# Dense products of a split float32 weight: the weights' low part as the last pass of each half block

## The chip, the cores and the metric

The kernel runs on one core of one Trainium2 chip. The metric is the device time of one execution in microseconds, over several runs, as their median. Engines are named as the profile names them: PE is TensorE (PEld its weight loads), DVE VectorE, ACT ScalarE, POOL GpSimd, SP SyncE, which issues nearly all DMAs.

## The reference

Two transformer-like blocks run one after the other on 512 positions of 2048 channels. The first has a depthwise convolution branch and a differential attention branch; the second mixes a gated delta rule (GDN, 8 heads) and an RWKV-7 recurrence (16 heads, in pairs) over a context of 256 positions and then over the 512 latent positions. Cut to what matters here:

```
p = h @ w_in[l]                                   # block 1, all projections
x = x + gate * rms_norm((sig*y_conv + sig*y_attn) @ w_o[l], g_post[l])
u  = h  @ w_in_2 ;  uc = hc @ w_in_2              # block 2: latent and context
ya_c, ya = gdn_mixer(uc[..., :GDN_COLS], u[..., :GDN_COLS], ...)
yb_c, yb = rwkv_mixer(uc[..., GDN_COLS:], u[..., GDN_COLS:], ...)
x = x + gate * (concat([ya, yb]) @ w_out)
```

Everything is float32, and the kernel keeps that accuracy in its large products.

## The kernel before

All activations are stored with channels on the 128 partitions and positions along the free axis. A dense output of 128 channels by T positions (T is 512, or 256 for the context) is one call of `mblock` (lines 129 to 136): it takes one PSUM bank from the pool `pd`, which has two, and calls `products` once for each **half block** of eight input blocks of 128 channels. `products` (lines 139 to 158) loads the half block's weights into `wraw` (three buffers), and splits them: ACT copies them to `whi`, rounded to the fast matmul type fp32r (line 105), and DVE subtracts to get the rest, `wlo` (line 106). `whi` and `wlo` have two buffers each. The activations exist as the same kind of pair (`ah`, `al`), made earlier. Then come three matmuls for each of the eight input blocks, `whi*ah`, `whi*al`, `wlo*ah`, 24 in all, accumulated in one PSUM bank (line 157). In the stage of the context's dense GDN products `K.on_pool` is 2, so every second `wlo` is made by POOL in place of DVE.

The program is written in Python once and its order on each engine is set by a list scheduler ahead of time; each engine then runs its list strictly in order and waits on semaphores. The scheduler takes, of the instructions that its own plan holds to be ready, the one with the lowest priority number, which is by default the place in the program. Two things bend that. In `products` every matmul whose number n in the accumulation is not a multiple of `K.burst` (12 in the first part, 6 from the end of block 1 on) gets a priority that puts it ahead of all else, so dense products come in bursts of 6 or 12 and other PE work can only come in between bursts. And the class `Visit` (lines 113 to 126) does the same for the few matmuls of one step of a recurrence. So the dense products of the next head fill PE while the recurrence of the present head waits for DVE or ACT.

The stages, by the time in the profile: the first products of block 1, in six banks at once and a quarter of the inputs at a time (`block1_h`, up to about 145 us); convolution and gates (to 435); the context's dense GDN products (`ctx_dense_gdn`, to about 626); the context's recurrences and block 1's attention (to 1780); block 1's output products (to 2150); the latent GDN stage (`mixers_gdn`, about 2240 to 3000); the latent RWKV stage (`mixers_rwkv`, to about 3620); output products and the final norm.

The GDN recurrence of one head (`gdn_core`, line 735 on) is four steps, each a chain of three handovers between PE and DVE: PE multiplies the state (`pc<-S,gk`), DVE makes `gd_R` (line 747), PE multiplies (`pc<-gd_R,gd_uu`), DVE makes `gd_vn` (line 755), PE multiplies (`pc<-gd_vn,gd_ktl` and four matmuls into `po` for the output), DVE makes the next state `S` (line 775).

Of the kernel before, what the change touches and what calls it, by code (L numbers as in the profile page):

```python
# [103 lines left out]
def split(K, hi, lo, src, eng=None):  # L104
    K.nc.scalar.copy(hi, src)  # L105
    (eng or K.nc.vector).tensor_tensor(lo, src, hi.bitcast(F32), op=ALU.subtract)  # L106


FIRST = 1000000
# [22 lines left out]
def mblock(K, wap, act, T, k0=0, k1=16, half=8):  # L132

    ps = K.pd.tile([128, 512], F32, name="pd")
    for ka in range(k0, k1, half):
        products(K, ps, wap, act[ka - k0:], T, ka, min(half, k1 - ka), k0, k1)
        K.fill()
    return ps[:, :T]


def products(K, ps, wap, act, T, ka, w, k0, k1):


    nc, tc = K.nc, K.tc
    raw = K.wp.tile([128, 8, 128], F32, name="wraw")
    hi = K.wp.tile([128, 8, 128], F32R, name="whi", bufs=2)
    lo = K.wp.tile([128, 8, 128], F32R, name="wlo", bufs=2)
    nc.sync.dma_start(raw[:, :w], wap[:, ka:ka + w, :])
    K.n_split += 1
    split(K, hi[:, :w], lo[:, :w], raw[:, :w], nc.gpsimd if K.on_pool and K.n_split % K.on_pool == 0 else nc.vector)  # L150
    for k in range(w):
        ah, al = act[k]
        for j, (a, b) in enumerate(((hi, ah), (hi, al), (lo, ah))):
            n = 3 * (ka - k0 + k) + j
            ahead = FIRST if n % K.burst else 0
            tc.cur_priority -= ahead
            nc.tensor.matmul(ps[:, :T], lhsT=a[:, k], rhs=b, start=(n == 0), stop=(n == 3 * (k1 - k0) - 1))  # L157
            tc.cur_priority += ahead


def rsqrt(K, pool, src, shape, a, eps, name, eng=None, exact=False):
# [196 lines left out]
def inv64(K, pool, upool, nm, ds, px, tmp):  # L358
# [30 lines left out]
    for lev in range(2):  # L389
        yp, zp = products()  # L390
        ys = pool.tile([128, n, 32], F32, name="iv_y")
        for m in range(n):
            for r in range(4):
                q = slice(32 * r, 32 * r + 32)
                o = 32 * (r % 2)
                nc.tensor.matmul(yp[q, m], lhsT=nm[q, m, o:o + 32], rhs=t32[q, m], start=True, stop=True,
                                 tile_position=(32 * r, 32 * r))
        nc.scalar.copy(ys, yp)
        for m in range(n):
            for r in range(4):  # L400
                q = slice(32 * r, 32 * r + 32)
                nc.tensor.matmul(zp[q, m], lhsT=ys[q, m], rhs=u32[q, m], start=True, stop=True,  # L402
                                 tile_position=(32 * r, 32 * r))
        for d, m0, w in orders:
            nc.vector.copy_predicated(u32[:, m0:m0 + w], K.cp[d, lev].unsqueeze(1).to_broadcast([128, w, 32]),  # L405
                                      zp[:, m0:m0 + w])
        nc.vector.transpose(t32.rearrange("p n e -> p (n e)"), u32.rearrange("p n e -> p (n e)"))

    u64 = upool.tile([128, n, 64], F32, name="iv_u64")
    for b in range(2):  # L410
        nc.vector.tensor_scalar(u64[:, :, 32 * b:32 * b + 32], u32, c["m64"][:, b:b + 1], None, op0=ALU.mult)
    yp, zp = products()
    ys = pool.tile([128, n, 32], F32, name="iv_y")

# [1432 lines left out]
```

## Time and profile before

| | us |
|---|---|
| median of 3 runs | 3961.03 |
| lowest and highest | 3956.98 and 3964.54 |
| the profiled execution's own time | 3948.75 |
| its span, first to last instruction | 3947.0 |
| PE busy in it | 3672.7 |
| DVE busy in it | 2748.4 |
| ACT busy in it | 1359.4 |
| POOL busy in it | 505.4 |

The profile shows one execution. Matmuls overlap: a product of 512 columns is shown with about 0.39 us, though one starts every 0.23 us. "Idle before" is the time in which an engine had nothing to run, and its releaser is what ended that time. A tile name stands for all its buffers. In the profile the two names before a matmul's size are the tensor that moves and the one that is loaded as weights, so `pd<-big,wlo` is a product of the weights' low part with an activation in `big`, and `hc` holds the context's activations.

### The profile page before, as it was taken

To read this page: it belongs to the slowest core of one execution; us is meant where nothing else is said; L and a number is where in the kernel's file an instruction comes from. 1 tells how busy PE (TensorE), PEld (TensorE's weight loads), DVE (VectorE), ACT (ScalarE), POOL (GpSimd) and SP (SyncE) were. 2 spreads that over 40 slices of the span, in tenths; PEclk is the share of its full clock that TensorE was granted. 3 is DMA by queue.
4 is the path that set the end of the run, shared out by engine and by line. 5 is a ranking of instruction groups with operands and counts; after the bars stand their busy time and mean duration, and the time that the engine had idled before them with its cause. 6 is when DMAs were issued, how large, how long until landed. Compare 5 with 4: busy or idle time off the path is not lost. (4 is left out here: it accounts for less than half of the span.)

```text
span 3947.0 us, 81802 instructions
## 1 busy us (share of the span) xinstructions
PE 3672.7 (93%) x33066; PEld 2837.3 (72%) x33066; DVE 2748.4 (70%) x7146; ACT 1359.4 (34%) x2713; POOL 505.4 (13%) x595
## 2 busy tenths in 40 slices
PE   8899878999999999999998889989999999998997
PEld 4577678876777777777886577777877777766676
DVE  3366798788778778553524877776767778877866
ACT  3322333323334344332322432322323444444333
POOL 0100231003101001000311201100001111111102
PEclk9999899999999999999999999999999999999998
DMA  8766445423433333425523222222223122212235
GB/s 321 269 226 216 161 133 173 140 102 127 136 118 107 118 111 126 130 81 179 204 93 129 101 88 68 67 69 75 86 79 110 65 68 81 68 67 83 91 129 203
DMA packets 206491, 492.95 MB, mean 125 GB/s; under 512 B 40096, under 2 KB 71328, under 8 KB 202016
## 3 DMA queue, kind: packets, MB, share of 16 engines
q1 hardware_dynamic: 206112, 487.72, 36.4%
q8 instruction: 260, 4.26, 0.4%
q14 instruction: 119, 0.97, 0.1%
HBM read 434.54 MB, written 53.09 MB: 124 GB/s over the span
## 5 line engine op out<-in xcount | busy, mean ns | idle before, releaser
L157 PE MATMUL pd<-big,whi 128*128 128x512 f32 x5280 | 1759.5, 411 | 8.0 <-ACT big L352 8.0
L157 PEld LDWEIGHTS pd<-big,whi 128*128 128x128 f32 x5280 | 964.4, 192 | 251.4 <-issue 20.8
L157 PE MATMUL pd<-big,wlo 128*128 128x512 f32 x2768 | 1104.2, 399 | 24.3 <-DVE wlo L106 23.6
L105 ACT CAST whi<-wraw 128x1024 fp32r<-128x1024 f32 (+2 forms) x498 | 502.9, 1010 | 1159.5 <-PE pd L157 1074.7
L106 DVE TENSOR_TENSOR wlo<-wraw,whi 128x1024 fp32r<-128x1024 f32 (+2 forms) x478 | 572.9, 1199 | 318.4 <-ACT whi L105 311.2
L157 PEld LDWEIGHTS pd<-big,wlo 128*128 128x128 f32 x2768 | 530.0, 191 | 147.1 <-DVE wlo L106 28.2
L157 PE MATMUL pd<-hc,whi 128*128 128x256 f32 x1152 | 227.0, 297 | 11.5 <-ACT hc L352 5.5
L157 PE MATMUL pd<-hc,wlo 128*128 128x256 f32 x576 | 171.7, 298 | 33.0 <-DVE wlo L106 23.9
L157 PEld LDWEIGHTS pd<-hc,whi 128*128 128x128 f32 x1152 | 188.3, 199 | 15.3 <-ACT hc L352 5.6
L157 PE MATMUL pd<-ext,whi 128*128 128x512 f32 x512 | 184.6, 401 | 3.8 <-DVE ext L106 3.8
L1160 DVE SCALAR_TENSOR_TENSOR cv_y<-cv_up,vec,cv_y 128x512 f32<-128x512 f32 x240 | 180.9, 754 | 4.2
L157 PE MATMUL pd<-fa,whi 128*128 128x512 f32 x448 | 149.9, 414 | 0.9 <-ACT fa L105 0.8
L157 PEld LDWEIGHTS pd<-hc,wlo 128*128 128x128 f32 x576 | 114.8, 199 | 40.0 <-DVE wlo L106 28.0
L944 POOL TENSOR_TENSOR rg_bk<-rg_th,rg_L 64x512 f32<-64x512 f32 x48 | 69.1, 1439 | 400.5 <-ACT rg_L L923 274.0
L1055 ACT ACTIVATE rg_zw<-rg_H,rg_wc 64x64 f32<-64x64 f32 x320 | 102.8, 342 | 43.4 <-DVE rg_H L1077 39.2
L157 PEld LDWEIGHTS pd<-ext,whi 128*128 128x128 f32 x512 | 97.3, 190 | 27.9 <-DVE ext L106 4.7
L1077 DVE SCALAR_TENSOR_TENSOR rg_H<-pc,rg_wc,rg_zw 64x64 f32<-64x64 f32 x320 | 90.4, 282 | 33.7 <-PE pc L123 24.0
L567 DVE SCALAR_TENSOR_TENSOR gc_y<-gc_up,vec,gc_y 128x512 f32<-128x512 f32 (+1 forms) x160 | 108.6, 679 | 2.8 <-issue 0.2
L242 DVE SCALAR_TENSOR_TENSOR ada_ev<-wraw,cs_ada,ada_ev 128x512 f32<-128x512 f32 x120 | 93.7, 781 | 20.3 <-DMA wraw<-in_wada_dram 18.9
L157 PEld LDWEIGHTS pd<-fa,whi 128*128 128x128 f32 x448 | 80.7, 190 | 21.8 <-ACT fa L105 1.9
L157 PE MATMUL pd<-fa,wlo 128*128 128x512 f32 x224 | 89.1, 398 | 0.7 <-DVE wlo L106 0.7
L405 DVE COPY_PREDICATED iv_u<-cpi,px 128x256 f32<-128x256 int32 (+2 forms) x112 | 35.2, 340 | 73.2 <-PE px L402 62.8
(589 smaller groups left out, 5592.9 us busy)
## 6 DMA issues: line engine op xcount, KB each, us to landing
wraw<-in_w_dram SPq DMA_DIRECT2D x366, 512.0 KB, 3.6
wraw<-in_wada_dram SPq DMA_DIRECT2D x128, 512.0 KB, 4.5
wraw<-in_wada_dram SPq DMA_DIRECT2D x32, 1024.0 KB, 4.8
wraw<-in_wo_dram SPq DMA_DIRECT2D x32, 512.0 KB, 3.5
sgl<-sgd SPq DMA_DIRECT2D x48, 256.0 KB, 3.3
wraw<-in_wout_dram SPq DMA_DIRECT2D x20, 512.0 KB, 3.8
wraw<-in_w_dram SPq DMA_DIRECT2D x36, 256.0 KB, 3.6
sgd<-msg SPq DMA_DIRECT2D x32, 256.0 KB, 3.3
```

The lines of the kernel that those rows point to most:

```text
L105: K.nc.scalar.copy(hi, src)
L106: (eng or K.nc.vector).tensor_tensor(lo, src, hi.bitcast(F32), op=ALU.subtract)
L157: nc.tensor.matmul(ps[:, :T], lhsT=a[:, k], rhs=b, start=(n == 0), stop=(n == 3 * (k1 - k0) - 1))
L242: nc.vector.scalar_tensor_tensor(ev, raw[:, k], cs[:, kk, 0:1], ev, op0=ALU.mult, op1=ALU.add)
L405: nc.vector.copy_predicated(u32[:, m0:m0 + w], K.cp[d, lev].unsqueeze(1).to_broadcast([128, w, 32]), zp[:, m0:m0 + w])
L567: nc.vector.scalar_tensor_tensor(y, up[:, t:t + T], w[:, t:t + 1], y, op0=ALU.mult, op1=ALU.add)
L944: nc.gpsimd.tensor_tensor(bk[uq, :, u], th[uq], F[uq], op=mul)
L1055: nc.scalar.activation(zw[hv[u], d], H[hv[u], ms[d], u], AF.Copy, scale=wn[hv[u], 4 * d + mn])
L1077: nc.vector.scalar_tensor_tensor(Hn[hv[u], 4 * d + mn, u], pc3[hv[u], 2, d], wn[hv[u], 4 * d + mn], zw[hv[u], d], op0=mul, op1=ALU.add)
L1160: nc.vector.scalar_tensor_tensor(y, up[:, t:t + 512], w[:, t:t + 1], y, op0=ALU.mult, op1=ALU.add)
```

## The change

In `products` the loop over input blocks with three products each is replaced by one list: first `whi*ah` and `whi*al` for every input block, then `wlo*ah` for every input block. Products, operands and their number stay the same; so do loads, splits and buffers. The number n still counts through the list, so a burst ends after the same number of matmuls. The new matmul stands at line 156.

```diff
-    for k in range(w):
-        ah, al = act[k]
-        for j, (a, b) in enumerate(((hi, ah), (hi, al), (lo, ah))):
-            n = 3 * (ka - k0 + k) + j
-            ahead = FIRST if n % K.burst else 0
-            tc.cur_priority -= ahead
-            nc.tensor.matmul(ps[:, :T], lhsT=a[:, k], rhs=b, start=(n == 0), stop=(n == 3 * (k1 - k0) - 1))
-            tc.cur_priority += ahead
+    n = 3 * (ka - k0)
+
+    for a, k, b in [(hi, k, b) for k in range(w) for b in act[k]] + [(lo, k, act[k][0]) for k in range(w)]:
+        ahead = FIRST if n % K.burst else 0
+        tc.cur_priority -= ahead
+        nc.tensor.matmul(ps[:, :T], lhsT=a[:, k], rhs=b, start=(n == 0), stop=(n == 3 * (k1 - k0) - 1))
+        tc.cur_priority += ahead
+        n += 1
```

What the scheduler makes of it is seen in the order of instructions. First, PE in the context's dense GDN products, around a norm's `px<-gc_th` matmul. Before:

```order
L157 MATMUL pd<-hc,whi 128x256 x2
L157 MATMUL pd<-hc,wlo 128x256
L157 MATMUL pd<-hc,whi 128x256 x2
L157 MATMUL pd<-hc,wlo 128x256
L260 MATMUL px_4296<-gc_th,cst 128x256
L157 MATMUL pd<-hc,whi 128x256 x2
L157 MATMUL pd<-hc,wlo 128x256
```

and with the change:

```order
L156 MATMUL pd<-hc,whi 128x256 x16
L156 MATMUL pd<-hc,wlo 128x256 x8
L260 MATMUL px_4296<-gc_th,cst 128x256
L156 MATMUL pd<-hc,whi 128x256 x16
L156 MATMUL pd<-hc,wlo 128x256 x8
```

The first product that needs `wlo` stands 17th in a half block and no longer third; the other work of this stage stands where it stood.

Second, DVE in the latent GDN stage, second head, where `wlo` is made. Before, the head's `wlo` stands 27 rows behind the `gd_R` of the next head's first step, after `gd_dd`, `iv_tmp` and the output norm; the rows around it:

```order
L377 STREAM_SHUFFLE iv_sh<-iv_u_23237 128x32
L565 TENSOR_SCALAR gc_y<-gc_up,vec 128x512
L378 TENSOR_TENSOR iv_sh<-iv_sh,iv_n_23235 128x32
L106 TENSOR_TENSOR wlo<-wraw,whi 128x1024
L379 TENSOR_TENSOR iv_u_23237<-iv_u_23237,iv_sh 128x32
```

With the change:

```order
L747 SCALAR_TENSOR_TENSOR gd_R_23531<-pc,TM_lat,gd_vt 128x128
L173 SCALAR_TENSOR_TENSOR go_rs_t<-go_rs_y 128x4
L567 SCALAR_TENSOR_TENSOR gc_y<-gc_up,vec,gc_y 128x512
L174 TENSOR_TENSOR go_rs_t<-go_rs_t,go_rs_xh 128x4
L106 TENSOR_TENSOR wlo<-wraw,whi 128x1024
L175 SCALAR_TENSOR_TENSOR go_rs_y<-go_rs_t,go_rs_y 128x4
```

One `wlo` now stands four rows behind that `gd_R`, ahead of `gd_dd`, `iv_tmp` and the output norm.

Third, PE in the recurrence of the third head, from the outputs of the first step on. Before:

```order
L123 MATMUL po<-gd_egt,S_0_5734 128x128
L157 MATMUL pd<-big,whi 128x512 x2
L157 MATMUL pd<-big,wlo 128x512
L157 MATMUL pd<-big,whi 128x512 x2
L157 MATMUL pd<-big,wlo 128x512
L123 MATMUL pc<-S_23550,gk 128x128
L123 MATMUL pc<-S_23548,gk 128x128
L309 MATMUL px_23759<-cst,gn_rs_y 4x128
L157 MATMUL pd<-big,whi 128x512 x2
L157 MATMUL pd<-big,wlo 128x512
L157 MATMUL pd<-big,whi 128x512 x2
L157 MATMUL pd<-big,wlo 128x512
```

With the change:

```order
L123 MATMUL po<-gd_egt,S_0_5734 128x128
L123 MATMUL pc<-S_23550,gk 128x128
L123 MATMUL pc<-S_23548,gk 128x128
L123 MATMUL pc<-gd_R_23559,gd_uu 128x128
L123 MATMUL pc<-gd_R_23557,gd_uu 128x128
L309 MATMUL px_23759<-cst,gn_rs_y 4x128
L315 MATMUL px_23762<-gc_th,cst 128x128 x2
L123 MATMUL pc<-gd_vn_23566,gd_ktl 128x128
L123 MATMUL pc<-gd_vn_23564,gd_ktl 128x128
```

In this head the dense products stand in one longer run ahead of the recurrence, and its handovers follow each other without a burst between them.

## Rows read from the trace of the kernel before

**Rows 1.** The page's parts 1 and 2: busy time, and slices of PE and its clock.
```profile
PE 3672.7 (93%) x33066; PEld 2837.3 (72%) x33066; DVE 2748.4 (70%) x7146; ACT 1359.4 (34%) x2713; POOL 505.4 (13%) x595
...
PE   8899878999999999999998889989999999998997
...
PEclk9999899999999999999999999999999999999998
```
**Rows 2.** The page's part 5, dense products of `wlo`, by the activation's tile.
```profile
L157 PE MATMUL pd<-big,wlo 128*128 128x512 f32 x2768 | 1104.2, 399 | 24.3 <-DVE wlo L106 23.6
...
L157 PE MATMUL pd<-hc,wlo 128*128 128x256 f32 x576 | 171.7, 298 | 33.0 <-DVE wlo L106 23.9
```
**Rows 3.** Waits of PE, whole span: us in total, times, longest us.
```profile
PE pd L157 <- DVE wlo L106: 48.1, 24, 4.5
...
PE pd L157 <- POOL wlo L106: 8.8, 14, 2.0
...
PE pc L157 <- DVE wlo L106: 0.6, 1, 0.6
...
PE px L157 <- DVE wlo L106: 0.5, 1, 0.5
```
**Rows 4.** Windows: the context's dense GDN stage and the latent GDN stage.
```profile
456.00:626.00 170.00, 134.58 (x976) 126.69 (x975) 148.58 (x290) 60.41 (x95) 56.08 (x57) 0.94 0.41 134
...
2240.00:3000.00 760.00, 712.11 (x6708) 578.62 (x6707) 549.14 (x1640) 227.57 (x400) 70.89 (x165) 0.97 0.25 82
```
**Rows 5.** Waits of PE from 456 to 626 us.
```profile
PE pd L157 <- DVE wlo L106: 23.6, 15, 4.3
```
**Rows 6.** Waits of PE from 2240 to 3000 us.
```profile
PE pd L157 <- DVE wlo L106: 22.6, 5, 4.5
PE pc L123 <- DVE gd_vn L755: 7.1, 6, 1.2
```
**Rows 7.** Timeline of PE in a latent GDN head: start, us, instruction.
```profile
2405.31 0.63 PE L157 MATMUL pd<-big,whi 128*128 128x512 f32 x2
2405.78 0.39 PE L157 MATMUL pd<-big,wlo 128*128 128x512 f32 x1
2406.01 0.63 PE L157 MATMUL pd<-big,whi 128*128 128x512 f32 x2
2406.47 0.39 PE L157 MATMUL pd<-big,wlo 128*128 128x512 f32 x1
...
2410.06 0.73 PE L157 MATMUL pd<-big,whi 128*128 128x512 f32 x2
2415.30 0.79 PE L157 MATMUL pd<-big,wlo 128*128 128x512 f32 x1 [4.50 <-DVE wlo L106]
...
2416.74 0.63 PE L157 MATMUL pd<-big,wlo 128*128 128x512 f32 x1
...
2418.02 0.59 PE L157 MATMUL pd<-big,wlo 128*128 128x512 f32 x1
```
**Rows 8.** Timelines of ACT and DVE around the same wait.
```profile
2408.85 1.04 ACT L105 CAST whi<-wraw 128x1024 fp32r<-128x1024 f32 x1 [0.90 <-PE pd L157]
...
2414.03 1.22 DVE L106 TENSOR_TENSOR wlo<-wraw,whi 128x1024 fp32r<-128x1024 f32 x1
```
**Rows 9.** Windows behind that wait: PE's instructions (x7) and granted clock 0.50.
```profile
2415.30:2418.40 3.10, 3.10 (x7) 2.47 (x8) 3.10 (x9) 0.00 (x0) 0.00 (x0) 0.50 0.53 176
```
**Rows 10.** Timelines of DVE and POOL in the context's dense GDN stage.
```profile
558.74 0.42 DVE L174 TENSOR_TENSOR gn_t<-gn_t,gn_xh 128x256 f32<-128x256 f32 x1
...
561.33 2.50 DVE L174 TENSOR_TENSOR gn_t<-gn_t,gn_xh 128x256 f32<-128x256 f32 x1
...
560.34 3.21 POOL L106 TENSOR_TENSOR wlo<-wraw,whi 128x1024 fp32r<-128x1024 f32 x1 [1.24 <-ACT whi L105]
```
**Rows 11.** Timeline of PE, a GDN handover with no product between.
```profile
2386.75 0.61 PE L123 MATMUL pc<-gd_R,gd_uu 128*128 128x128 f32 x4
2388.53 0.71 PE L123 MATMUL pc<-gd_vn,gd_ktl 128*128 128x128 f32 x4 [1.18 <-DVE gd_vn L755]
```
**Rows 12.** Timeline of PE at the start of a stage whose activations are just being split.
```profile
1789.18 0.79 PE L157 MATMUL pd<-ext,whi 128*128 128x512 f32 x1 [3.77 <-DVE ext L106]
```

## Prediction

> **What bounds the kernel.** I read the page's parts 1 and 2 first. PE is busy 93% of the span, and near 9 tenths in most slices; no other engine comes near [rows 1]. So time is saved where PE stops, or where its clock falls. Next came the costliest groups: there the products of `wlo` carry nearly all idle time of the dense products, 24.3 us for the latent ones and 33.0 us for the context's [rows 2]. The waits of PE agree: it stood 48.1 us in 24 stops for a `wlo` of DVE, 8.8 us in 14 for one of POOL, and 1.1 us more, 58.0 us in all [rows 3]. That is 1.5% of the span, and the most that the change can hand back directly.
>
> Then I asked where these stops lie. Two stages hold 55.0 of the 58.0 us: the context's dense GDN products (23.6 us for DVE's, and POOL's 8.8) [rows 3, 5] and the latent GDN stage, where five stops take 22.6 us [rows 6]. These two are not alike. In the latent stage PE is busy 712.1 of 760 us and DVE 549.1; in the context's stage it is the other way round, PE 134.6 of 170 us and DVE 148.6 [rows 4]. What a removed stop is worth must be read from each.
>
> A third thing is the price of a stop beyond itself. In a steady run a `wlo` product stands every 0.69 to 0.70 us, 0.23 us per product; behind the stop of 4.50 us they stand 1.28 and 1.44 us apart, 0.43 to 0.48 us per product [rows 7]. The granted clock there is 0.50, which is the 1.2 GHz level, and PE did nothing ahead of it for the length of the stop [rows 7, 9].
>
> **The change part by part.** It adds and removes no instruction, and no load or split. What it moves is when `wlo` is first needed, when `whi` is free again, and, through the scheduler, the order on all engines.
>
> *Latent GDN, the stops.* PE came to the third product of a half block, while ACT had cast `whi` at 2408.85 and DVE made `wlo` only at 2414.03, behind its other work in the queue [rows 8]. Now 16 products need `whi` alone, so `wlo` may be 14 products later: 14 x 0.23 = 3.2 us. The other 1.3 us of a stop should go too, as the order shows a `wlo` far earlier in DVE's list, and `whi` is released after two thirds of a half block. I take all five stops: -22.6 us [rows 6].
>
> *Latent GDN, the clock.* Seven matmul records ran at the low clock behind each stop [rows 9]. Each cost 0.43 - 0.23 = 0.20 us more, so 5 x 7 x 0.20 = -7.0 us.
>
> *Latent GDN, the handovers.* This speaks against the change. In the order of this stage I count 185 runs of dense products before and 157 with the change, for almost the same number of products (1926 and 1902). PE has fewer places where a burst covers a handover of the recurrence to DVE and back. Handovers without a product between go from 17 to 39, 22 more. A bare one cost 1.18 us of PE's time [rows 11], and six of that kind 7.1 us [rows 6]. Of the 22, four more have nothing between; the others have two to five small matmuls, or the output's four, in the gap. From below such a one costs 0: before, eleven handovers of this kind left no row among this stage's longer waits, where the six empty ones did [rows 6]; from above it costs 1.18 us. I take 1.18 us for four and half, 0.6 us, for 18: 4.7 + 10.8 = +15.5 us, between 4.7 and 26.0. On the other side a run that starts anew costs about 0.10 us (its first two products 0.73 us, in a run 0.63) [rows 7], and 28 fewer starts give -2.8 us. The stage comes to -22.6 - 7.0 + 15.5 - 2.8 = -16.9 us.
>
> *Context's dense GDN.* PE's 32.4 us of stops lie beside a DVE that idles only 170 - 148.6 = 21.4 us [rows 4], and every handover of the stage passes DVE. So no more than 21.4 us can come back here as long as DVE's work keeps its length, and none need to, if DVE only waits elsewhere. I take half, -10.7 us. What holds DVE is seen in one row: a `gn_t` multiplication of 0.42 us took 2.50 us while POOL made a `wlo` for 3.21 us [rows 10], and nothing here takes that away. The Trainium skill says on its page "SBUF — State Buffer", section "Who interferes with whom", that VectorE's second SBUF input comes through a read interface shared with GpSimd, and that such instructions contend. The row agrees: the time lost is DVE's, not PE's, and by that rule alone this stage would give 0 and the sum come out 10.7 us later.
>
> *The remaining stops*: 58.0 - 22.6 - 32.4 = 3.0 us, in many places [rows 3]; I take them all, -3.0 us.
>
> *Starts of stages.* Where activations are split just ahead of the products, as at 1789.18, where PE waited 3.77 us for one [rows 12], the last activation is now followed by 2 + 8 products of its half block instead of 3: 7 x 0.23 = 1.6 us later. The four chunks of block 1's first products and the four ahead of the latent stage have half that many products, and others of the same chunk beside them. I take +4.0 us for all, between 0 and 8.
>
> *SP, the DMAs and POOL*: a half block's load moves by a few places in SP's list, and is hidden by the two half blocks that its third buffer holds ahead; without that cover it would show as a wait for `wraw`, which no row here has. POOL makes the same 20 `wlo`, with the two small `gc_up` fills behind each as before. 0 for both.
>
> The sum is -16.9 - 10.7 - 3.0 + 4.0 = -26.6 us. Against the profiled execution's 3948.75 us that is 3922.2 us. That execution lies 12.3 us (0.3%) below the median of the runs shown, 3961.03 us, and under the lowest of them; the runs are what the change is compared with, so the forecast is 3961.03 - 26.6 = 3934 us.
>
> **The rivals.**
> - *Everything comes back.* The bare handovers cost little, since the small matmuls in them fill the gap, and DVE's idle time is all used: -22.6 - 7.0 + 4.7 - 2.8 - 21.4 - 3.0 = -52.1 us, 3909 us. For it: 18 of the 22 have something between. Against it: DVE already stood between PE's two matmuls in the one bare handover that I can read [rows 11].
> - *DVE bounds the context's stage and the handovers are dear.* GDN gives -22.6 - 7.0 + 26.0 - 2.8 = -6.4, the context's stage 0, remaining stops -3.0, starts +4.0: -5.4 us, 3956 us, within what can be told from no change. For it: DVE's held `gn_t` [rows 10], and PE's price in [rows 11].
> - *Slower: DVE's queue paces a bare recurrence.* In the third and fifth head the recurrence now runs from the first step's output to its end without products, while DVE's list still has 0.7 to 1.2 us instructions, a `wlo` of 1.22 us among them [rows 8], between the links. If a handover then costs its 1.18 us and one such instruction, 2.4 us, the 22 cost 52.8 us. The stage gives +20.4 us, the starts 8.0, the context's stage and the rest nothing: +28.4 us, 3989 us. It decides from about (22.6 + 7.0 + 2.8) / 22 = 1.5 us per handover in this stage. Against it: the row of 1.18 us already has DVE's other work in it, as five of its kind came out the same [rows 6].
> - *The change does not do what it says*: ruled out for the context's stage by the order; in six-bank work bursts are mixed with those of other banks, but `wlo` stands late there too.
>
> **How the numbers follow.** I give the forecast (from -45 to -10 us) 0.62, everything back 0.10, the dear handovers with DVE as bound 0.18, slower 0.10. The predicted time is the likeliest, 3934 us. The range reaches from a little beyond everything back, 3902 us, to a little beyond the case without a gain, 3964 us; outside lie the slower rival and some of the first, about 0.15. A difference under 0.2%, 8 us, can't be told from no change here. Faster by more than that hold the forecast, the first rival and a few of the second: 0.76. Within it: the larger part of the second, 0.14. Slower: 0.10.
>
> **What would show it.** In the profile of the changed kernel PE's stops for `wlo` should be under 10 us in all; the five of 4.5 us in the latent GDN stage gone, and the slices of low clock behind them. That stage should take about 743 us. Waits of PE for `gd_R`, `gd_vn` and `S` should rise from 7 to some 20 us; over 40 us would be the slower rival. The context's dense GDN stage should be 5 to 20 us shorter, with DVE's idle time there under 12 us; if it is as long as before, DVE was its bound. The dense products' number and pace, 0.23 us, should be as before; another pace, or a longer RWKV stage through its changed order, would make the prediction wrong for a cause that I have not priced.

## The result, and the profile after

The changed kernel took 3985.95 us in the median of 5 runs (3983.73 to 3992.44), beside 3961.03 us of the kernel before on the same chip (5 runs, 3945.15 to 3970.88). The ratio is 1.007, 95% interval 1.0043 to 1.0097: slower, by some 25 us, where I forecast 27 us faster. The two profiled executions lie further apart, with spans of 3990.7 and 3947.0 us; where the text compares stages by them, the runs below say what is left of it.

First the whole, PE's busy time, its slices and its clock, to be held against [rows 1], and the span with the mean granted clock:

```profile
PE 3723.3 (93%) x33066; PEld 2871.8 (72%) x33066; DVE 2743.2 (69%) x7146; ACT 1367.6 (34%) x2713; POOL 501.8 (13%) x595
...
PE   8899879999999999999998799999999999999997
...
PEclk9999989999999999999999999999999998899898
```

```profile
core 0: 3990.7 us, clock 0.950
```

PE is as full as before, but the mean clock is 0.950, where the kernel before had 0.962. There are two levels, 2.4 and 1.2 GHz, so the time at the lower one is 2 x (1 - 0.950) x 3990.7 = 399 us against 2 x (1 - 0.962) x 3947.0 = 300 us. These some 100 us more, at half the pace, are worth up to some 50 us; the spans differ by 43.7.

What was to go did go. The dense products of `wlo`, with their idle time last, as in [rows 2] (line 156 now):

```profile
L156 PE MATMUL pd<-big,wlo 128*128 128x512 f32 x2768 | 743.5, 403 | 0.0
...
L156 PE MATMUL pd<-hc,wlo 128*128 128x256 f32 x576 | 83.0, 288 | 7.0 <-DVE wlo L106 6.7
```

The stops fell from 58.0 us to some 7. But PE's waits over the whole span (us in total, times, longest) show others beside the three stops for DVE's `wlo` that are left of [rows 3]:

```profile
PE px L260 <- ACT gc_th L572: 17.4, 6, 3.9
...
PE px L518 <- DVE gg_R L488: 13.7, 2, 7.2
...
PE pd L156 <- DVE wlo L106: 6.7, 3, 3.4
...
PE pc L123 <- DVE gd_vn L755: 5.0, 8, 0.9
...
PE pc L123 <- DVE gd_R L747: 2.5, 5, 0.7
...
PE pc L123 <- DVE S L775: 1.6, 4, 0.6
...
PE po L123 <- DVE gd_vn L755: 1.4, 2, 0.7
```

The stop for `gc_th` is new, 17.4 us, and lies in the context's dense GDN stage. The one for `gg_R` was 7.2 us before; one of its two stops, 7.2 us, now lies in that stage too, where it took 0.8. So of PE's 32.4 us of stops there 7.0 are left and some 24 came back under other names. The handovers of the GDN recurrence (`gd_vn`, `gd_R`, `S`) make 10.5 us in all in these rows, far from the 52.8 us of my slower rival. Then the stages, by windows (length, busy time of PE, PEld, DVE, ACT and POOL, then the granted clock), the first and third against [rows 4], the fourth against a line of before that follows, the second against one shown with e18:

```profile
456.00:626.00 170.00, 134.18 (x994) 129.11 (x993) 151.07 (x294) 63.36 (x101) 55.06 (x58) 0.91 0.42 137
740.00:1640.00 900.00, 861.75 (x8504) 645.58 (x8503) 702.08 (x2039) 330.41 (x744) 106.43 (x128) 0.97 0.35 116
2240.00:3000.00 760.00, 724.17 (x6653) 590.66 (x6652) 541.42 (x1619) 229.13 (x389) 69.53 (x160) 0.96 0.25 83
3000.00:3620.00 620.00, 579.94 (x8009) 435.82 (x8009) 486.96 (x1454) 265.12 (x653) 91.94 (x78) 0.92 0.21 69
```

The fourth before:

```profile
3000.00:3620.00 620.00, 577.80 (x8237) 434.37 (x8235) 498.75 (x1487) 262.98 (x652) 87.01 (x74) 0.94 0.21 69
```

In the context's dense GDN stage PE is as busy as before, and DVE 2.5 us busier, with 18.9 us of idle time where it had 21.4; the clock is 0.91 where it was 0.94. Nor did the stage's pace change: the last five of its `px<-gc_th` matmuls (line 260) stand 16.1 us apart on average in the trace of before (553.3 to 617.8 us), and 16.0 now (552.1 to 616.2). In the latent GDN stage PE idles 12.1 us less, but the clock is lower. Between 740 and 1640 us, where the context's recurrences run beside block 1's attention, it was 0.98 before.

The same view asked for every 20 us and added up gives three stages in finer numbers (us; low is time at 1.2 GHz, worked out from the granted clock):

| | length, before / after | PE idle | low |
|---|---|---|---|
| 740 to 1640 us | same window | 30.9 / 38.2 | 27.6 / 51.2 |
| latent GDN, first head to first RWKV product | 664.7 / 664.6 | 36.8 / 25.0 | 34.0 / 51.6 |
| latent RWKV, to the last output products | 908.1 / 939.7 | 56.7 / 53.4 | 89.6 / 147.6 |

In the GDN stage 11.8 us less idle time and 17.6 us more at the low level, worth 8.8, nearly cancel. In the first row 7.3 us of idle time and half of 23.6 us at the low level come to 19 us, in the third 29 us come from the clock alone.

How the clock came down in the latent GDN stage is seen in PE's timeline of one head:

```profile
2548.30 0.71 PE L123 MATMUL pc<-S,gk 128*128 128x128 f32 x4 [0.57 <-DVE S L775]
2549.71 0.71 PE L123 MATMUL pc<-gd_R,gd_uu 128*128 128x128 f32 x4 [0.70 <-DVE gd_R L747]
...
2551.71 1.03 PE L123 MATMUL pc<-gd_vn,gd_ktl 128*128 128x128 f32 x4
...
2554.24 1.06 PE L123 MATMUL pc<-S,gk 128*128 128x128 f32 x4
...
2556.01 0.71 PE L123 MATMUL pc<-gd_R,gd_uu 128*128 128x128 f32 x4
2557.42 0.71 PE L123 MATMUL pc<-gd_vn,gd_ktl 128*128 128x128 f32 x4 [0.70 <-DVE gd_vn L755]
...
2559.23 0.71 PE L123 MATMUL pc<-S,gk 128*128 128x128 f32 x4 [0.21 <-DVE S L775]
...
2561.04 0.71 PE L123 MATMUL pc<-gd_R,gd_uu 128*128 128x128 f32 x4 [0.31 <-DVE gd_R L747]
2562.45 0.80 PE L123 MATMUL po<-gd_at,gd_vn 128*128 128x128 f32 x2 [0.70 <-DVE gd_vn L755]
...
2565.77 1.87 PE L837 MATMUL po<-cst,go_t 128*128 128x1 f32 x8 [1.24 <-ACT go_t L1130]
2567.50 2.91 PE L156 MATMUL pd<-big,whi 128*128 128x512 f32 x6
```

From 2547.7 us on there is not one dense product for some 20 us. PE runs the small matmuls of the recurrence and waits 0.2 to 1.2 us at most of its handovers. The windows of this stretch:

```profile
2547.70:2551.90 4.20, 2.55 (x15) 1.83 (x15) 2.88 (x15) 0.69 (x3) 0.00 (x0) 1.00 0.36 125
2551.90:2555.30 3.40, 3.40 (x17) 3.18 (x16) 0.60 (x2) 0.43 (x2) 0.00 (x0) 0.51 0.00 0
2555.30:2562.20 6.90, 5.22 (x37) 4.37 (x36) 6.66 (x17) 1.26 (x2) 3.24 (x3) 0.99 0.00 0
2562.20:2572.40 10.20, 8.70 (x29) 7.15 (x30) 5.04 (x27) 2.68 (x5) 1.08 (x6) 0.50 0.21 53
```

PE was busy 2.55 of 4.20 us, and then the clock stands at 0.51 for 3.4 us; PE is busy 5.22 of 6.90, and it stands at 0.50 for 10.2 us, the first dense products behind the recurrence among them. Before, PE stopped for `wlo` and then ran at the low level [rows 7, 9]; now it runs a bare recurrence and then does.

Something like it is seen in block 1, beside the context's RWKV recurrence:

```profile
1347.44 1.19 PE L156 MATMUL pd<-big,whi 128*128 128x512 f32 x4
1348.47 0.63 PE L156 MATMUL pd<-big,wlo 128*128 128x512 f32 x2
1349.03 0.45 PE L123 MATMUL pc<-rg_H,rg_bt 128*64 128x64 f32 x8
1349.41 1.66 PE L156 MATMUL pd<-big,wlo 128*128 128x512 f32 x6
1350.90 1.55 PE L156 MATMUL pd<-big,whi 128*128 128x512 f32 x6
1352.29 0.60 PE L1232 MATMUL po<-cst,at_s 128*128 128x128 f32 x4
1352.64 1.63 PE L156 MATMUL pd<-big,whi 128*128 128x512 f32 x6
1356.28 0.71 PE L970 MATMUL px<-cst,rg_bk 64*128 64x64 f32 x8 [2.01 <-POOL rg_bk L945]
```

Four bursts, 24 products, stand almost together, the second of them six low parts, and then PE has nothing to put beside the wait of 2.01 us for `rg_bk`. From 1357.3 us the clock is at its lower level for 6.8 us. This is one place; stops for `rg_bk` as such are not new, and the waits that did grow in this stage are shown with e2 below.

### The profile page after: what moved, and what is told of

Same layout as the page of the kernel before. It is cut to its first block, busy times and chain, and to the rows that moved or that the text cites. A ratio compares the mean times of both kernels' runs of the same rounds, so it can differ in the third digit from the quotient of the medians.

```text
span 3990.7 us, 81842 instructions
## 1 busy us (share of the span) xinstructions
PE 3723.3 (93%) x33066; PEld 2871.8 (72%) x33066; DVE 2743.2 (69%) x7146; ACT 1367.6 (34%) x2713; POOL 501.8 (13%) x595
## 5 line engine op out<-in xcount | busy, mean ns | idle before, releaser
L156 PE MATMUL pd<-big,whi 128*128 128x512 f32 x5280 | 1444.7, 410 | 10.0 <-ACT big L352 8.0
L156 PEld LDWEIGHTS pd<-big,whi 128*128 128x128 f32 x5280 | 978.6, 193 | 260.8 <-issue 28.1
L156 PE MATMUL pd<-big,wlo 128*128 128x512 f32 x2768 | 743.5, 403 | 0.0
L156 PE MATMUL pd<-hc,whi 128*128 128x256 f32 x1152 | 169.4, 299 | 10.2 <-ACT hc L352 5.3
L156 PE MATMUL pd<-ext,whi 128*128 128x512 f32 x512 | 166.6, 402 | 3.8 <-DVE ext L106 3.8
L156 PEld LDWEIGHTS pd<-hc,whi 128*128 128x128 f32 x1152 | 153.7, 201 | 15.6 <-ACT hc L352 5.7
L156 PE MATMUL pd<-fa,whi 128*128 128x512 f32 x448 | 131.0, 431 | 1.6 <-DVE wo L1555 1.1
L992 PE MATMUL px<-rg_C,rg_bk 64*128 64x128 f32 x512 | 87.5, 307 | 2.3 <-DVE rg_C L995 1.6
L156 PE MATMUL pd<-hc,wlo 128*128 128x256 f32 x576 | 83.0, 288 | 7.0 <-DVE wlo L106 6.7
L378 DVE TENSOR_TENSOR iv_sh<-iv_sh,iv_n 128x64 f32<-128x64 f32 (+2 forms) x336 | 82.1, 244 | 6.4
```

The lines of the kernel that those rows point to most:

```text
L378: nc.vector.tensor_tensor(sh, sh, n8[:, :, i:i + 1].to_broadcast([128, w, 8]), op=ALU.mult)
L992: nc.tensor.matmul(pg[:, m], lhsT=bk[q, 4 * r + m].rearrange("p x c -> p (x c)"), rhs=C[q, 4 * r + m, u], start=True, stop=True, tile_posi ...
```

## The experiments

All ratios are against runs of the kernel before on the same chip. `K.stage` is 1 up to the latent GDN stage (the products made ahead for it count as 1), 2 in that stage, 3 behind it. `third` is the old list of products, `late` the new one.

### Which stage holds the loss

Four kernels have the new order in one part each:

```diff
+    for a, k, b in (late if COND else third):
# e1: T == 256    e2: T == 512 and K.stage == 1    e3: K.stage == 2    e4: K.stage == 3
```

e1: 

> The new order of products only where T is 256 (the context's products), the old one for T of 512. Theory A (the scheduler's new order leaves PE sparser in the attention and RWKV stages, which then run longer at the 1.2 GHz level): this stage is bound by DVE, PE's 32 us of stops for wlo turn into other waits, so the time is that of before within 5 us; the end of the context's dense GDN stage comes 0 to 3 us earlier than before. Theory B (bare GDN handovers cost it): the same here, 0 to 5 us faster. My prediction's term was -10.7 us.

Measured: 0.9985 (0.9969 to 1.0), 6 us faster. In the profile the recurrence behind this stage begins 3.7 us earlier. A gain is likely, though the interval just reaches none.

e2: 

> The new order only for T of 512 ahead of the latent GDN stage: block 1 with its attention, beside which the context's RWKV runs. Theory A: 10 to 18 us slower than before, all of it between the first and the last attention product, with 25 to 40 us more at the low clock there. Theory B: 0 to 5 us faster, since no GDN handover of the latent stage is touched.

Measured: 1.0046 (1.0024 to 1.0067), 18 us slower. This is the largest part of the loss, as theory A had it. From 740 to 1640 us PE idles 41.1 us, where it idled 30.9, and the low level takes 55.2 us, added up as above, where it took 27.6. PE's waits in that window, two rows of before and then two of e2, show that it is not `rg_bk` that grew:

```profile
PE px L970 <- POOL rg_bk L945: 6.8, 4, 2.6
PE px L837 <- ACT r_sq L875: 0.6, 1, 0.6
```

```profile
PE px L973 <- POOL rg_bk L948: 3.9, 2, 2.0
PE px L840 <- ACT r_sq L878: 5.5, 3, 3.2
```

e3: 

> The new order only in the latent GDN stage. Theory A: the stops for wlo (22 us) go, but bare recurrences put the clock down for about 40 us more, so the stage is within 8 us of before. Theory B: 15 to 25 us slower, by waits of PE for gd_R, gd_vn and S of over 40 us in that stage. My prediction's term was -16.9 us.

Measured: 1.0005 (0.9987 to 1.0023). PE's waits for `gd_vn`, `gd_R` and `S` are 9.7 us in this stage. Theory B, my slower rival, is out, and so is my -16.9 us. In the profile the stage itself is 4.7 us shorter (660.0 us, PE idle for 26.2) with 38.0 us at the low level: 4.0 more than before, not theory A's 40. What is lost lies, in this profile, behind the stage: the RWKV stage takes 937.9 us, 165.2 of them at the low level. There the list of products is the old one, but PE's order, read from the trace, is not that of before.

e4: 

> The new order only in the latent RWKV stage and the output products. Theory A: 12 to 30 us slower than before, with 50 to 100 us more at the low clock from 3000 us on. Theory B: within 5 us of before.

Measured: 1.0007 (0.9987 to 1.0028), against theory A's 12 to 30 us. The 32 us by which the RWKV stage differs between the two first profiles are thus not the product order alone. The parts add up to +0.43%, or 17 us, against 1.007 for the whole; the intervals leave room for both that and something that they do only together.

Single profiles scatter, but every run has its mean granted clock on record. Over the 149 runs of the kernel before that stand beside the experiments, a run is 3.3 us longer for each 0.001 that its clock is lower (correlation -0.95). So a difference can be parted into what a run of the kernel before shows at that clock, and a rest (means of all runs, which differ from the ratios by a few us; 95% intervals):

| | difference, us | mean clock, this / before | with the clock | rest |
|---|---|---|---|---|
| e1 context | -5.2 | 0.9587 / 0.9599 | +4.1 | -9.3 ± 2.0 |
| e2 block 1 | +21.7 | 0.9559 / 0.9599 | +13.0 | +8.7 ± 2.3 |
| e3 latent GDN | +2.6 | 0.9552 / 0.9599 | +15.5 | -12.9 ± 1.2 |
| e4 latent RWKV | +4.1 | 0.9582 / 0.9599 | +5.7 | -1.6 ± 2.5 |
| all four, the change | +22.9 | 0.9512 / 0.9596 | +27.5 | -4.6 ± 3.4 |

The last row is against the 149 runs. Taken chip by chip the 3.3 us lie between 2.7 and 4.0, which moves a rest of e1 to e4 by 3.5 us at most. In e1 and e3 the waits that went are a sure gain, and the clock takes it back; in e2 it adds more than half of the loss. What lowered the clock, and in which stage, these means do not tell.

### Why block 1 lost, first round

Two kernels change block 1 alone, to part theories S, P and L:

```diff
# e5, T of 512, K.stage 1
+    early = late[:2] + late[2 * w:2 * w + 1] + late[2:2 * w] + late[2 * w + 1:]
# e8, the order of e2, and in block1
-    K.burst = 6
+    K.burst = 3
```

e5: 

> Ahead of the latent GDN stage (T of 512) the low part of the first input block stays third, the other seven come last. Theory S (with the low parts last the scheduler holds a half block ready before its wlo is made, so it places products earlier and has none left where a recurrence waits): the third product needs wlo again, so the time is that of before within 6 us. Theory P (what counts is the place of the low parts, not when the half block is ready): 12 to 22 us slower, as with all eight last. Theory L (any other order of the list scheduler falls out differently, with no direction): anything from -15 to +25 us, unlike both.

Measured: 1.0034 (1.0013 to 1.0055), 13 us slower. This speaks against theory S, since `wlo` is needed as early as before; the interval's low end, 5 us, would still fit it.

e8: 

> The new order only for T of 512 ahead of the latent GDN stage, and a burst of 3 in place of 6 from the gates of block 1 on (315 runs of products in PE's order there, 273 before, 275 with the new order and 6). Theory S: finer bursts cover the recurrences beside the attention again, and the 18 us that the new order cost here come down to under 8 us. Theory P or L: no such return, 10 to 30 us slower, with 40 more starts of runs at about 0.1 us in it.

Measured: 1.004 (1.0021 to 1.0059), 16 us slower. Finer bursts don't bring it back.

e11 is its control, the old list with `K.burst = 3` there: 

> The old order of products, and bursts of 3 in block 1 from its gates on; only the scheduler's order there changes (308 runs of products against 273). Theory L (the order before falls out well here, and nearly any other is 10 to 20 us slower through waits and low clock beside the recurrences): 8 to 20 us slower, although no low part is moved. Theory P (the place of the low parts costs it): within 6 us of before.

Measured: 1.0 (0.9987 to 1.0014). This other order of the scheduler costs nothing, which speaks against theory L and for the place of the low parts.

### Bursts in the latent GDN stage

```diff
# e6, old list; e7, new list where K.stage is 2; e10, old list
# e6
+    ahead = FIRST if K.stage == 2 else 0
+    tc.cur_priority -= ahead
     split(K, hi[:, :w], lo[:, :w], raw[:, :w], ...)
+    tc.cur_priority += ahead
# e7 and e10, ahead of mixers_gdn
-        K.burst = 6
+        K.burst = 3
```

e6: 

> The old order of products everywhere; in the latent GDN stage the two instructions that make whi and wlo get the priority that puts them ahead of all else. This takes the stops for wlo away without touching the products' order. It also cuts the runs of products of this stage in PE's order from 178 to 148, as the new order does (151). Theory S: the stops go (-22 us), longer runs leave recurrences bare, so waits and low clock take most of it back: within 6 us of before, as with the new order in this stage. If my prediction's price of a bare handover (0.6 us) were right: 12 to 20 us faster.

Measured: 1.0032 (1.001 to 1.0054), 13 us slower than before, with no stop for `wlo` among that stage's waits. Its handovers, in PE's waits from 2240 to 3000 us:

```profile
PE pc L124 <- DVE S L780: 5.6, 5, 1.1
PE pc L124 <- DVE gd_vn L760: 5.5, 5, 2.3
PE pc L124 <- DVE gd_R L752: 3.0, 5, 0.7
```

So one can take the stops away without the new order, and still lose: 30 fewer runs of products, 14.1 us of waits in the recurrence, and from the first head to the first RWKV product 673.2 us in place of 664.7, with 48.4 us at the low level where 34.0 were.

e7: 

> The new order in the latent GDN stage alone, with a burst of 3 products in place of 6 there, which brings the runs of products back to 179 (178 before, 151 with the new order and 6). Theory S: the stops are gone and the recurrences are covered again, so the stage is 10 to 22 us shorter than before and the low clock there under 20 us; the whole 5 to 20 us faster, less what the moved products leave to the RWKV stage. Rival (the stops' time is needed by DVE anyway): within 4 us of before.

Measured: 0.9978 (0.9964 to 0.9992), 9 us faster. The stage itself takes 655.1 us in place of 664.7, with PE idle for 19.0 us; but the low level takes 52.0 us, not under 20.

e10: 

> The control of the run before with bursts of 3: the old order of products, and bursts of 3 in the latent GDN stage. The stops for wlo should be there again, at least 10 us of them. Theory S (cover of the recurrence and late low parts are both needed): 0 to 6 us slower or faster than before, so the gain of 8 us there is the new order's. Rival (finer bursts alone gave it): 6 to 12 us faster than before.

Measured: 0.9953 (0.9935 to 0.997), 19 us faster. The rival is right, and the stops, which I expected back, are not there, in PE's waits from 2240 to 3000 us (line 158 in this kernel):

```profile
PE pd L158 <- DVE wlo L107: 1.7, 2, 1.4
```

The stage takes 646.6 us, PE idles 22.7 us in it and runs 21.6 us at the low level. So the 22.6 us of [rows 6] were no price of the old order of products by itself: with bursts of 3 they go too. Why, in DVE's list, no run shows. With the old order the finer bursts give some 10 us more than with the new one (e7), by intervals that barely meet.

### Parts together

```diff
# e9: late where T == 256 or K.stage == 2;  e12: and where K.stage == 3;  both K.burst = 3 in stage 2
# e13: late where T == 256, K.burst = 3 in stage 2;  e16: and in stage 3
```

e9: 

> The two parts that gained, together: the new order in the context's products and in the latent GDN stage, there with bursts of 3; the old order in block 1 and in the RWKV stage. If the parts add up: 0.9985 x 0.9978, 0.9963 of before, some 15 us faster, 3948 us. If what a stage gains is given back by the next through the changed order and clock: within 5 us of the GDN part alone, 8 us faster.

Measured: 0.9985 (0.997 to 1.0), less than the sum of 0.9963, though the intervals of the parts leave room for it. Parted as above, the rest is -18.9 us, near e1's -9.3 and e7's -13.1 together, and the clock costs 10.3.

e12: 

> The whole change but for block 1, with bursts of 3 in the latent GDN stage. If block 1 holds the loss of the change and the RWKV stage costs nothing sure: 5 to 18 us faster than before. If the RWKV stage holds a part of it (32 us between the two first profiles): 0 to 15 us slower.

Measured: 1.0043 (1.0023 to 1.0063), 0.6% more than e9, from which it differs in the RWKV stage alone. That stage is 26.6 us longer in the profile, and its low level takes 162.0 us against 108.8. Alone (e4) the same list cost nothing there. So what the list costs in this stage depends on what comes ahead of it; 18.5 of the 25.7 us between the means of e9 and e12 go with the clock.

e13: 

> A kernel that may beat both: the new order in the context's products alone, the old one elsewhere, bursts of 3 in the latent GDN stage. If the parts add up (0.9985 and 0.9953): 0.9938, some 24 us faster than before. If the gain of the context's part is given back: 16 to 20 us faster, as with bursts of 3 alone.

Measured: 0.9952 (0.9929 to 0.9975), 3941.81 us, like e10. Either beats both kernels, by 19 us the one before. That the context's part adds to it is not shown in the time; in the rest beside the clock it is, -26.6 us against e10's -17.6, with e1's -9.3.

e16: 

> As the first of this group, with bursts of 3 in the latent RWKV stage too. If finer bursts cover the RWKV recurrences as they did those of GDN: 5 to 20 us faster than the first of this group, with less time at the low clock from 3000 us on. If that stage is bound by its own chains: within 5 us of it, or slower by the more starts of runs.

Measured: 1.0048 (1.0025 to 1.007), 38 us slower than e13. What helps GDN harms the RWKV stage.

### Why block 1 lost, second round

```diff
# T of 512, K.stage 1
# e14
+    hold = late[:2 * w - 1] + late[2 * w:] + late[2 * w - 1:2 * w]
# e15: of each two input blocks four whi products, then two of wlo
# e17, the order of e2
-        ahead = FIRST if n % K.burst else 0
+        ahead = FIRST if n % K.burst or (K.stage == 1 and T == 512 and n % 24 == 18 and w == 8) else 0
# e18: of each four input blocks eight whi products, then four of wlo
```

e14: 

> Ahead of the latent GDN stage (T of 512) the low parts come late as with the change, but the last of the 16 whi products is held back behind them, so whi comes free where it did before. Theory H (the earlier release of whi costs it): within 6 us of before. Theory G (the eight low parts in one block cost it): 10 to 20 us slower, as with the change in this stage.

Measured: 1.007 (1.0046 to 1.0094), 28 us slower. The release of `whi` is not the cause.

e15: 

> Ahead of the latent GDN stage (T of 512) the low parts come last within each burst of six (four whi products, two of wlo). whi comes free one product earlier than before. Theory H and theory G both: within 6 us of before. If it is 8 to 20 us slower, any move of the low parts costs time in this stage, and neither names the cause.

Measured: 1.0006 (0.9985 to 1.0026).

e17: 

> Ahead of the latent GDN stage (T of 512) all low parts last, as with the change, but no new burst may begin at the 19th product of a half block (bursts of 6, 6 and 12), so that in PE's order one burst begins with a low part in place of 56; 252 runs of products against 275. Theory K (bursts that begin with a low part cost it): within 6 us of before, or some us slower by the coarser last burst. Theory G (eight low parts in a row): 12 to 25 us slower, as with the change in this stage.

Measured: 1.0017 (1.0002 to 1.0031), 7 us slower, 11 less than e2, although its runs of products are fewer and longer.

e18: 

> Ahead of the latent GDN stage (T of 512) the low parts come last within each four input blocks (eight whi products, four of wlo), bursts of 6 as before; one burst begins with a low part. Theory K: within 6 us of before. Theory G, taken as a cost that grows with how late the low parts are: 6 to 14 us slower, between e15 (0.0006 of the time) and all eight last (0.0046).

Measured: 0.9998 (0.9984 to 1.0012). From 740 to 1640 us, before, then e2, then e18:

```profile
740.00:1640.00 900.00, 869.10 (x8516) 652.07 (x8517) 710.53 (x2066) 335.64 (x759) 101.10 (x128) 0.98 0.36 118
```

```profile
740.00:1640.00 900.00, 858.88 (x8447) 642.78 (x8445) 695.54 (x2023) 328.29 (x735) 105.46 (x128) 0.97 0.36 115
```

```profile
740.00:1640.00 900.00, 867.39 (x8524) 651.00 (x8523) 711.92 (x2057) 331.71 (x753) 106.03 (x128) 0.98 0.37 118
```

PE is busy 869.10, 858.88 and 867.39 us; the low level, added up as above, takes 27.6, 55.2 and 42.0 us, so one profile alone would not have told e18 from a slower kernel. Set side by side with the bursts of PE's order that begin with a low part, from the end of the context's dense products to the latent GDN stage:

| block 1 | bursts that begin with `wlo` | ratio | with the clock, us | rest, us |
|---|---|---|---|---|
| before | 2 | 1 | 0 | 0 |
| e11 old list, bursts of 3 | 1 | 1.0 | -1.7 | +0.6 |
| e15 low parts last in six | 1 | 1.0006 | -1.8 | +3.1 |
| e18 low parts last in twelve | 1 | 0.9998 | +0.8 | -1.7 |
| e17 all last, bursts 6, 6, 12 | 1 | 1.0017 | +4.1 | +1.9 |
| e5 one low part third | 56 | 1.0034 | +8.8 | +5.8 |
| e8 all last, bursts of 3 | 70 | 1.004 | +9.8 | +8.0 |
| e2 all last | 56 | 1.0046 | +13.0 | +8.7 |
| e14 all last, but one `whi` | 62 | 1.007 | +14.7 | +7.6 |

e17 and e2 have the same list of products and differ in one place where a burst may begin; by the midpoints it takes away more than half of the loss. So in this stage it goes mostly with the bursts that begin with a low part, and what is left, at most 12 us by e17's interval, may be the block of eight. That the four kernels with such bursts lose both by the clock and beside it is shown by all their runs, in the last two columns. Single profiles cannot show it for each: idle and low time from 740 to 1640 us are 32.5 and 45.2 us in e5, which lost 13 us, and 39.9 and 34.8 in e15, which lost nothing. How such a burst leads the scheduler to leave recurrences bare is not shown.

## Why the prediction was wrong

- *The stops.* Right that they would go: 58.0 us became some 7. Wrong that they come back as time.
- *Latent GDN, the stops and the clock* (-22.6 and -7.0 us). This is one of two steps that failed, by some 19 us: -16.9 us for the stage, and +2 measured (e3, between -5 and +9). I took the stops as the cause of the low clock and let the clock recover with them. PE's idle time did fall by 11.8 us, but time at the low level rose by 17.6, some of it behind bare recurrences: the clock's term was +8.8 us in this profile. In e3's it was +2.0 in the stage, and more came in the RWKV stage behind it; over all runs of e3 the clock's part is +15.5 us against a gain of 12.9 beside it. The -7.0 was also mis-sized from the start: it counts seven records behind each stop, where the stage had 34.0 us at the low level, worth up to 17.
- *Latent GDN, the handovers* (+15.5 us). The waits for `gd_vn`, `gd_R` and `S` in this stage are 9.4 us where six waits of 7.1 us stood in [rows 6], so as waits I priced them too high. The clock behind them was not in the step. The 22.6 us were, by e10, not tied to the order of products.
- *Context's dense GDN* (-10.7 us). -6 us, between 0 and -12 (e1); beside the clock -9.3, and the clock took some 4 back. I had written that DVE's idle time would fall under 12 us; it fell from 21.4 to 18.9, and in place of 32.4 us for `wlo` PE waits 17.4 us for `gc_th` and 7.2 for `gg_R` there, at an unchanged pace of 16 us. The sign agrees, and the rule of the Trainium skill, page "SBUF — State Buffer", section "Who interferes with whom", by which the stage alone would give 0, lies at the upper end of that interval; a run did not part the two. The unchanged pace speaks for 0, the -9.3 us beside the clock for my term.
- *The remaining stops and the starts of stages* (-3.0 and +4.0 us). This is the other step that failed, by some 17 us: for block 1 and the RWKV stage I counted stops and starts only, and took their changed order as free. Block 1 alone cost 18 us (e2), more than half of it with the lower clock. I had named a longer RWKV stage as unpriced, and thus had a hole where the loss was; the stage that I had not named was the surer one.
- *The slower rival* had the sign and nearly the size (3989 us), by luck: its mechanism is refuted by the waits and e3.
- *Pace*: unchanged, 0.23 us between products at the high level.

What stays open is the RWKV stage: 32 us longer in the first profile, nothing by the new order alone (e4), 0.6% between e9 and e12. In ten of the kernels (e1, e2, e5, e6, e8, e11, e14, e15, e17 and e18) PE's order in that stage is the one of before, read from the traces. With before's own profile that makes eleven of one order; they lie between 908 and 933 us, 918 on average, and before's is the shortest. So some 10 of the 32 us are the luck of one profile, and a single profile of this stage can't be read to better than 25 us. e3 (937.9) and the changed kernel (939.7) lie above all eleven.

## What to carry to other kernels

Where a list scheduler fills one engine's gaps with dense work, an edit that makes the dense work ready earlier is first a change of where that work lands; count, for every stage, the stretches that it leaves without dense work, and price them with the granted clock and not only with the waits. The mean clock of each run parts the two better than one profile does. A stop that a trace shows may be a symptom of that order, and the size of a burst may remove it more cheaply than its operands' order (e10). Time an edit stage by stage and whole, since what one stage gains the clock may take back in the next (e3, e12).

## What the runs showed of the hardware

In the latent GDN stage the lower level of the clock came behind bare recurrences as it came behind full stops [rows 9]: after a stretch in which PE was busy 5.22 of 6.90 us, all in small matmuls, it stood for 10.2 us. Over the 20 profiled executions of this study the span goes with the mean granted clock (correlation -0.78), from 3931.9 us at 0.964 (e10) to 3995.1 us at 0.953 (e14), at nearly the same count of matmuls. The runs of the kernel before alone spread from 3945 to 3990 us, and there the time goes with the clock still more closely: -0.95 over 149 runs, with mean clocks from 0.952 to 0.965.
